# The embedding's product of an attention layer, computed as two products of 64 rows on the two halves of the array

## The chip, the core and the metric

The kernel runs on one core of a Trainium2 chip. The metric is the device time of one execution in microseconds, as the median of several runs; the shorter the better.

## What is computed

One layer: multi-head latent attention with a gated output, and then a per-layer embedding that is gated by the residual stream. All is float32; 1024 tokens, width 1024, an embedding of width 256. The end of it, with which this document deals, is

```
y = mla_mixer(h, cos, sin, ...)              # ends with (o * silu(z)) @ w_out
x = x + y
gate = jax.nn.sigmoid(rmsnorm(x) @ ple_gate[i])
x = x + gate * (p[i] @ ple_proj[i])          # p: 1024 x 256, ple_proj: 256 x 1024
return rmsnorm(x, final_norm)
```

## The kernel before

Tokens are cut into 8 row tiles of 128, features into chunks of 128 partitions. A product in float32 is the sum of three products of exact parts: with a = hi + lo, hi rounded to float32r, it is hi * hi + hi * lo + lo * hi (`pairs` lists the three). So every chunk of 128 contracted features costs three matmuls for each stretch of up to 512 output columns, and each matmul has its own weight load.

The phases are: projections of x, the gate silu(z), attention by pairs of heads, and the last phase from line 695: the out projection (lines 763 to 784) and then, for one row tile after the other, gate, embedding and norm (lines 786 to 819). Only this last loop is touched. For row tile t it does the following.

- `gate_lhs(t + 1)` makes the next tile's stationary operands: the residual `xs` transposed, as `aTh` and `aTl`, and the embedding `p_t`, as `ph` and `pl` (line 759 by way of line 91). From tile 2 on the transposition is made by VectorE and ScalarE, 32 x 32 blocks at a time (`xb`) which are then copied to their places (`xt`, line 132), then cast (line 746) and subtracted (line 91). The buffers of `aTh`/`aTl` alternate between even and odd tiles, so a cast waits until TensorE has done with the tile two before.
- Two halves i of 512 columns: 24 gate matmuls (8 chunks x 3) into a half of `ps_big`. After the first half come the embedding's matmuls for both halves, 2 chunks x 3 x 2 = 12, into two PSUM banks `ps_pj`. The stationary operand is `ph` or `pl`, the moving one a row of `w_p`.
- For each half: ScalarE's sigmoid from `ps_big` into `sg` (line 801), VectorE's `sg = ps_pj * sg` (line 802) and `xs += sg` (line 803), ScalarE's mean square (line 116).
- The norm: `rsqrt` in three Newton steps on VectorE (lines 96 to 107), the scaling of two halves on VectorE (line 817), the output by SyncE's queue.

The last row tile is cut into columns of 512, 256 and 256, and ScalarE scales one of its halves (line 815).

What stands first on an engine is decided by the scheduler of the framework when the program is built: it reorders each engine's instructions, and at run time each engine keeps that order and waits on semaphores. The transposition for a later tile thus stands between the gating steps of an earlier one. All PSUM tiles of one bank (`ps_tr`, `ps_o`, `ps_pj`) share four buffers.

Of the kernel before, what the change touches and what calls it, by code (L numbers as in the profile page):

```python
# [9 lines left out]
F32 = mybir.dt.float32  # L10
# [7 lines left out]
P = 128  # L18
# [10 lines left out]
PLE = 256  # L29
# [16 lines left out]
def _cut(v, bits):  # L46
    """v rounded to a multiple of 2**-bits."""
    return math.floor(v * 2.0 ** bits + 0.5) / 2.0 ** bits
# [3 lines left out]
def mla_ple_kernel(ctx, tc, x, x_t, p_t, pos, norm_g, w_c, w_z, q_norm, w_q, w_r, kv_norm, w_k, w_v,  # L52
                   w_out, ple_proj, ple_gate, final_norm, out):
    """One multi-head latent attention layer with a per-layer embedding gate.

    Products in float32 are carried as sums of exact float32r parts: a = hi + lo with hi = a
    rounded to float32r and lo = a - hi, so that hi*hi + hi*lo + lo*hi has float32's accuracy.
    """
    nc = tc.nc
# [33 lines left out]
    def rsqrt(v, n, name="rs_y", bufs=None):  # L93
        """1 / sqrt(v) of n columns, by Newton's method."""
        half = small.tile([P, n], I32, tag=f"rs_i{n}", name="rs_i", bufs=2)
        V.tensor_scalar(out=half, in0=v.bitcast(I32), scalar1=1, scalar2=None,
                        op0=ALU.logical_shift_right)
        y = small.tile([P, n], F32, tag=f"{name}{n}", name=name, bufs=bufs)
        V.tensor_scalar(out=y.bitcast(I32), in0=half, scalar1=-1, scalar2=0x5F3759DF,
                        op0=ALU.mult, op1=ALU.add)  # L100
        t = small.tile([P, n], F32, tag=f"rs_t{n}", name="rs_t", bufs=2)
        if n == 1:
            h = small.tile([P, 1], F32, tag="rs_h", name="rs_h", bufs=2)
            V.tensor_scalar(out=h, in0=v, scalar1=-0.5, scalar2=None, op0=ALU.mult)
            for _ in range(3):
                V.tensor_scalar(out=t, in0=y, scalar1=y, scalar2=h, op0=ALU.mult, op1=ALU.mult)
                V.scalar_tensor_tensor(out=y, in0=t, scalar=1.5, in1=y, op0=ALU.add, op1=ALU.mult)
            return y
        for _ in range(3):
            V.scalar_tensor_tensor(out=t, in0=y, scalar=-0.5, in1=y, op0=ALU.mult, op1=ALU.mult)  # L110
            V.tensor_tensor(out=t, in0=t, in1=v, op=ALU.mult)
            V.scalar_tensor_tensor(out=y, in0=t, scalar=1.5, in1=y, op0=ALU.add, op1=ALU.mult)
        return y
# [4 lines left out]
    def transposes(dst, src, n):  # L118
        """dst[:, 128 j + r] = src[r, 128 j + :] for n tiles."""
        for j in range(n):  # L120
            nc.tensor.transpose(dst[:, j * P:(j + 1) * P], src[:, j * P:(j + 1) * P], ident)  # L121

    def block_transposes(src, tmp):
        """src's 128 x 128 tiles transposed by 32 x 32 blocks, which are then moved to their rows."""
        n = src.shape[1]
        blk, dst = (z[:, :n] for z in tmp)
        V.transpose(out=blk, in_=src)
        b, d = (z.rearrange("p (k q n) -> p q k n", q=4, n=32) for z in (blk, dst))
        for i in range(4):
            for j in range(4):  # L130
                copy = A.copy if (i + j) % 4 == 1 else V.tensor_copy
                copy(out=d[i * 32:(i + 1) * 32, j], in_=b[j * 32:(j + 1) * 32, i])
        return dst.rearrange("p (k n) -> p k n", n=P)
# [8 lines left out]

    # z^T takes the place of what the first phase reads only once
    zst = ExitStack()
    zT_pool = zst.enter_context(pool("zT"))
    zT = zT_pool.tile([P, KT, S], F32, name="zT")

    # keeps the tensor engine awake while the first loads are under way
    idle = zT[:, 4, :256].bitcast(BF16)
# [16 lines left out]

    # ---------------------------------------------------------------- h, c_q, c_kv, k_rope
    uph = ExitStack()
# [23 lines left out]

    # x^T goes in unscaled: c_q and c_kv are normed anyway, k_rope and z are scaled afterwards
    def load_xT(t, ks=slice(0, KT)):
# [8 lines left out]
    def u_tile(t):  # L203
# [6 lines left out]
        for k in range(KT):  # L210
            for a, b in pairs:
# [4 lines left out]
                nc.tensor.matmul(pk, st, mv[:, k, QL:], start=first, stop=last)  # L216
        # the squares' means are those of c / r, so EPS is divided by r * r with 1 / r / r = msx + EPS
        un = unb[t % 3]
# [47 lines left out]
    def angles():  # L266
        """cos and sin of the positions' angles."""
        rp = uph.enter_context(pool("rope"))
# [15 lines left out]
        def nearest(o, i, s):  # L284
# [6 lines left out]
                        in1=inv.unsqueeze(1).broadcast_to([P, NT, HF]), op=ALU.mult)  # L291
        # the angle is a0 + 4096 (m0 + 1024 m1): a0 loses its turns in radians, m0 and m1 in turns
        nearest(m, ang, 1.0 / 4096)
# [33 lines left out]
        unwind(ang)  # L327
        # half the angle lies within a quarter turn: sin a = 2 s c, cos a = 1 - 2 s s
        ts1(ang, ang, 0.5, ALU.mult)
# [38 lines left out]

    # ---------------------------------------------------------------- silu(z)^T
    att1 = late.enter_context(pool("att1", side="right"))  # L370
# [36 lines left out]
    def project_r(g, hf):  # L407
        """x cos and x sin of four heads, left in DRAM for the rows that they go to."""
        cols = slice(hf * 512, hf * 512 + 512)
        if hf == 0:  # L410
            rq_of[g] = [tc.dram_tile([2, P, S], F32, name=f"rq{g}{z}") for z in "hl"]
        ps = product_q(wr_of[g], hf)
        t = rt_tile("rt").rearrange("p (c n) -> p c n", c=2)
        for n in range(2):
            V.tensor_tensor(out=t[:, n, :], in0=ps, in1=cs[n][:, cols], op=ALU.mult)
        hi = rh_tile("rh").rearrange("p (c n) -> p c n", c=2)
        lo = t.bitcast(F32R)
        A.copy(out=hi, in_=t)
        sub_hi(G, lo, t, hi)
        for z, d in zip((hi, lo), rq_of[g]):  # L420
            nc.gpsimd.dma_start(out=d.rearrange("c p n -> p c n")[:, :, cols], in_=z.bitcast(F32))

    # With q = [x1, x2] and the rotated key [k1, k2], the rotary score is
    # [x1 cos, x2 cos] . [k1, k2] + [x1 sin, x2 sin] . [k2, -k1].
    # The key's 64 rows go on either half, next to the even and the odd heads' other features.
    def rope_key():
# [22 lines left out]
    def spread(src, dst, n):  # L449
        """dst[n m + r, 128 t + :] = src[:, t, r], for 32 rows r or fewer that come over and over."""  # L450
        t, blk = rt_tile("spread"), rh_tile("blk").bitcast(F32)
# [13 lines left out]
    zph = ExitStack()  # L465
    # 1 / rms of x, along the tokens on every partition
    zr = zph.enter_context(pool("zr", reuse_waits="tile"))
# [36 lines left out]

    # ---------------------------------------------------------------- attention
    atts = ExitStack()
    att = atts.enter_context(pool("att"))
    # P^T of two blocks of queries; the last key tile lacks the first block, and stays empty there.
    # Few key tiles share the end of the buffer of many.
    pt_w = [[att.tile([P, n, 2 * P], F32R, name=f"pt{n}{z}") for z in "hl"] for n in (4, 8)]  # L510
# [22 lines left out]
    def odd_k():  # L533
        """The keys of a pair's second head, once those of the pair before are done with."""
        A.copy(out=k_hi[1][NOPE:], in_=kst[NOPE:])
# [60 lines left out]
    def normalise(c, alloc, eng):  # L596
        """The heads of pair c are divided by their sums, brought along the tokens through DRAM."""
        l = sums.pop(c)
# [95 lines left out]

    # ---------------------------------------------------------------- out projection, gate, norm
    fw1 = ctx.enter_context(pool("fw1", side="right", reuse_waits="tile"))
# [24 lines left out]
    def product(ps, st, w, nk, spans):  # L721
        for k in range(nk):
            for a, b in pairs:
                for o, cols in zip(ps, spans):
                    nc.tensor.matmul(o, st[a][:, k, :], w[k][b][:, cols],  # L725
                                     start=k == 0 and a + b == 0, stop=k == nk - 1 and a == 1)

    def out_lhs(t):
# [57 lines left out]
    for t in range(NT):  # L786
# [4 lines left out]
        spans = [slice(*z) for z in zip(edges, edges[1:])]  # L791
        pp = [ps_pj()[:, :z.stop - z.start] for z in spans]
        ms = small.tile([P, 3], F32, tag="ms2", name="ms2", bufs=2)
        for i, cols in enumerate(spans):
            n = cols.stop - cols.start
            po = ps_tr()[:, :n] if i == 2 else ps[:, cols]
            product([po], gl, w_g, KT, [cols])
            if i != 1:
                product(pp[i:i + 2], pl, w_p, PLE // P, spans[i:i + 2])
            sg = fin.tile([P, 512], F32, tag="sg", name="sg", bufs=2)[:, :n]  # L800
            A.activation(out=sg, in_=po, func=AF.Sigmoid, scale=r2[t])
            V.tensor_tensor(out=sg, in0=pp[i], in1=sg, op=ALU.mult)
            V.tensor_tensor(out=xs[:, t, cols], in0=xs[:, t, cols], in1=sg, op=ALU.add)  # L803
# [66 lines left out]
```

## Time and profile before

| | us |
|---|---|
| median of 3 runs | 727.88 |
| lowest and highest run | 727.80, 728.51 |
| span of the profiled execution | 726.3 |
| TensorE busy in that span | 707.7 |
| VectorE busy | 543.8 |
| ScalarE busy | 400.4 |
| GpSimd busy | 198.4 |

The page gives the profiled execution by its span, from the first instruction to the last; its time as the runs have it isn't on it. The busy share of an engine is a mean over phases with different limits. What a change in the last phase is worth is read there: from the chain of work that ended last, from the order in time on each engine with the idle time ahead of an instruction, and from busy times by stretch. In the names, PE is TensorE, PEld its weight loads, DVE VectorE, ACT ScalarE, POOL GpSimd.

### The profile page before, as it was taken

To read this page: it belongs to the slowest core of one execution; us is meant where nothing else is said; L and a number is where in the kernel's file an instruction comes from. 1 tells how busy PE (TensorE), PEld (TensorE's weight loads), DVE (VectorE), ACT (ScalarE), POOL (GpSimd) and SP (SyncE) were. 2 spreads that over 40 slices of the span, in tenths; PEclk is the share of its full clock that TensorE was granted. 3 is DMA by queue.
4 is the path that set the end of the run, shared out by engine and by line. 5 is a ranking of instruction groups with operands and counts; after the bars stand their busy time and mean duration, and the time that the engine had idled before them with its cause. 6 is when DMAs were issued, how large, how long until landed. Compare 5 with 4: busy or idle time off the path is not lost.

```text
span 726.3 us, 11589 instructions
## 1 busy us (share of the span) xinstructions
PE 707.7 (97%) x4031; PEld 614.0 (85%) x4031; DVE 543.8 (75%) x1364; ACT 400.4 (55%) x919; POOL 198.4 (27%) x208
## 2 busy tenths in 40 slices
PE   8999989999999999999999999998999999999995
PEld 7999768888988999888998899887878888888884
DVE  6996994334888988888888888899654258788854
ACT  6751333334777786777768777776553145333322
POOL 0000200223134533563345542165146142000000
PEclk9999999999999999999999999999999999999998
DMA  8710211324102403034120421033474020111101
GB/s 316 279 69 26 71 38 57 103 88 110 38 15 76 148 30 88 16 106 142 34 74 0 168 84 57 4 115 89 139 282 130 1 81 36 44 36 37 59 29 59
DMA packets 25675, 61.32 MB, mean 84 GB/s; under 512 B 4112, under 2 KB 8080, under 8 KB 25616
## 3 DMA queue, kind: packets, MB, share of 16 engines
q1 hardware_dynamic: 23168, 52.19, 22.7%
q0 software_dynamic: 2304, 8.39, 3.1%
q8 instruction: 32, 0.52, 0.3%
q14 instruction: 27, 0.22, 0.1%
q10 hardware_dynamic: 144, 0.00, 0.0%
HBM read 47.92 MB, written 12.65 MB: 83 GB/s over the span
## 4 chain that ended last, share of the span: by engine, by line
PE 86%; DVE 8%; ACT 2%; DMA 2%; issue 1%; SPq 0%; ACTq 0%; DVEq 0%
PE ps_big L725 22%; PE ps_big L583 13%; PE ps_o L635 10%; PE ps_big L487 9%; PE ps_tr L121 8%; PE ps_pj L403 6%; PE ps_big L215 4%; PE ps_pj L725 3%; PE ps_pj L544 3%; PE ps_pj L527 3%; PE ps_big L216 3%; PE ps_o L215 1%; PE ps_pj L216 1%; DVE kt L443 1%; DMA wst<-in_w_out 1%
## 5 line engine op out<-in xcount | busy, mean ns | idle before, releaser
L725 PE MATMUL ps_big<-w,aTh 128*128 128x512 f32 (+1 forms) x480 | 139.1, 390 | 0.0
L725 PEld LDWEIGHTS ps_big<-w,aTh 128*128 128x128 f32 x480 | 89.5, 188 | 20.1
L593 ACT ACTIVATE prob<-ps_big,mx 128x384 f32<-128x384 f32 (+6 forms) x112 | 89.3, 797 | 16.3 <-DVE mx L588 15.6
L588 DVE TENSOR_REDUCE mx<-ps_big 128x1 f32<-128x384 f32 (+6 forms) x112 | 91.6, 818 | 1.8
L121 PE MATMUL ps_tr<-ident,prob 128*128 128x128 f32 x576 | 84.2, 273 | 1.8 <-ACT prob L593 1.8
L725 PE MATMUL ps_big<-w,aTl 128*128 128x512 f32 (+1 forms) x240 | 84.5, 390 | 0.0
L121 PEld LDWEIGHTS ps_tr<-ident,prob 128*128 128x128 f32 x576 | 68.4, 140 | 11.4 <-ACT prob L593 2.6
L91 DVE TENSOR_TENSOR pt8l<-ps_tr,pt8h 128x512 fp32r<-128x512 f32 (+3 forms) x128 | 71.0, 581 | 4.4 <-ACT pt8h L624 3.8
L583 PE MATMUL ps_big<-k_hi,qh 128*128 128x512 f32 (+2 forms) x176 | 67.7, 385 | 0.9 <-ACT prob L593 0.7
L641 POOL TENSOR_TENSOR zT<-o,zT 64x256 f32<-64x256 f32 x56 | 41.0, 734 | 93.6 <-DVE o L639 79.8
L624 ACT CAST pt8h<-ps_tr 128x512 fp32r<-128x512 f32 (+3 forms) x128 | 60.7, 508 | 4.8 <-PE ps_tr L121 4.3
L583 PE MATMUL ps_big<-k_lo,qh 128*128 128x512 f32 (+2 forms) x176 | 61.9, 352 | 0.0
L583 PE MATMUL ps_big<-k_hi,ql 128*128 128x512 f32 (+2 forms) x176 | 61.4, 349 | 0.0
L635 PE MATMUL ps_o<-pt8h,vals 128*128 128x256 f32 x224 | 57.5, 294 | 0.0
L635 PE MATMUL ps_o<-pt8l,vals 128*128 128x256 f32 x224 | 54.9, 282 | 0.0
L725 PEld LDWEIGHTS ps_big<-w,aTl 128*128 128x128 f32 x240 | 45.0, 188 | 10.2 <-POOL aTl L91 0.5
L479 ACT ACTIVATE zh<-zs,g_col 128x128 fp32r<-128x128 f32 x64 | 20.8, 396 | 50.5 <-DMA zs<-in_w_z 38.0
L487 PE MATMUL ps_big<-hT_hi,zl 128*128 128x512 f32 x128 | 41.3, 404 | 4.1 <-DVE zl L480 4.1
L116 ACT ACTIVATE jk<-xs 128x512 bf16<-128x512 f32 (+2 forms) x25 | 18.8, 750 | 44.2 <-DVE xs L803 36.7
L635 PEld LDWEIGHTS ps_o<-pt8l,vals 128*128 128x128 f32 x224 | 42.8, 191 | 0.0
L635 PEld LDWEIGHTS ps_o<-pt8h,vals 128*128 128x128 f32 x224 | 42.6, 190 | 0.0
L624 ACT CAST pt4h<-ps_tr 128x384 fp32r<-128x384 f32 (+3 forms) x64 | 27.1, 425 | 27.4 <-PE ps_tr L121 27.2
(269 smaller groups left out, 1737.7 us busy)
## 6 DMA issues: line engine op xcount, KB each, us to landing
zT<-in_x SPq DMA_DIRECT2D x8, 512.0 KB, 4.9
zs<-in_w_z SPq DMA_DIRECT2D x16, 256.0 KB, 2.7
rlb<-rl SPq DMA_DIRECT2D x32, 128.0 KB, 3.1
wst<-in_w_out SPq DMA_DIRECT2D x8, 512.0 KB, 4.4
xs<-in_x SPq DMA_DIRECT2D x8, 512.0 KB, 7.2
wst<-in_ple_gate SPq DMA_DIRECT2D x8, 512.0 KB, 3.7
out<-xs SPq DMA_DIRECT2D x16, 256.0 KB, 2.0
zT<-in_x_t SPq DMA_DIRECT2D x6, 512.0 KB, 4.1
```

The costliest lines, as they stand in the source:

```text
L91: eng.tensor_tensor(out=lo, in0=src, in1=hi.bitcast(F32), op=ALU.subtract)
L121: nc.tensor.transpose(dst[:, j * P:(j + 1) * P], src[:, j * P:(j + 1) * P], ident)
L215: nc.tensor.matmul(pq, st, mv[:, k, :QL], start=first, stop=last)
L403: nc.tensor.matmul(ps, w[b][:, k, :], (cq_hi, cq_lo)[a][:, k, hf * 512:hf * 512 + 512], start=k == 0 and a + b == 0, stop=k == n - 1 and a ...
L487: nc.tensor.matmul(ps[:, hf * 512:(hf + 1) * 512], wz[k][b], (hT_hi, hT_lo)[a][:, k, hf * 512:(hf + 1) * 512], start=k == 0 and a + b == 0 ...
L583: nc.tensor.matmul(ps[:, off + s0:off + s1], q[a][:, qs], (k_hi, k_lo)[b][e][:, s0:s1], start=a + b == 0, stop=a == 1)
L588: V.tensor_reduce(out=mx, in_=s, axis=AX.X, op=ALU.max, negate=True)
L593: A.activation(out=pr[:, :n], in_=s, func=AF.Exp, bias=mx, scale=1.0, accum_out=l)
L624: A.copy(out=hi[:, j0:j0 + n, half], in_=src)
L635: nc.tensor.matmul(ps[:, :256], w, z[:, j, :], start=j + n == 0, stop=j == last and n == 1)
L641: (V if h >= H - 2 else G).tensor_tensor(out=z, in0=o[top], in1=z, op=ALU.mult)
L725: nc.tensor.matmul(o, st[a][:, k, :], w[k][b][:, cols], start=k == 0 and a + b == 0, stop=k == nk - 1 and a == 1)
```

## The change

For row tiles 0 to 6, a new function `by_halves` takes the place of `product` for the embedding, and is called once for each half of the columns, so it follows the gate's matmuls of either half. It makes two sums in two PSUM banks: the first from partitions 0 to 63 of each chunk, the second from partitions 64 to 127, a matmul of 64 rows for the one and for the other in turn. The matmuls are built as tiles of 64 x 128 of the array, at row 0 and at row 64. The two sums are joined behind the gate: VectorE multiplies the second by `sg` into `sg2`, GpSimd adds that to `xs`, then VectorE multiplies the first by `sg` and adds it. The last row tile stays as it was. The diff also strips comments, which moves line numbers.

```diff
+    def by_halves(st, w, nk, cols):
+        ps = [ps_pj(), ps_pj()]
+        for k in range(nk):
+            for a, b in pairs:
+                for e in range(2):
+                    r = slice(e * P // 2, (e + 1) * P // 2)
+                    nc.tensor.matmul(ps[e], st[a][r, k, :], w[k][b][r, cols],
+                                     start=k + a + b == 0, stop=k == nk - 1 and a == 1)
+        return ps
...
-        pp = [ps_pj()[:, :z.stop - z.start] for z in spans]
+        pp = [ps_pj()[:, :z.stop - z.start] if last else None for z in spans]
...
             product([po], gl, w_g, KT, [cols])
-            if i != 1:
-                product(pp[i:i + 2], pl, w_p, PLE // P, spans[i:i + 2])
+            if last:
+                if i != 1:
+                    product(pp[i:i + 2], pl, w_p, PLE // P, spans[i:i + 2])
+            else:
+                pp[i] = by_halves(pl, w_p, PLE // P, cols)
             sg = fin.tile([P, 512], F32, tag="sg", name="sg", bufs=2)[:, :n]
             A.activation(out=sg, in_=po, func=AF.Sigmoid, scale=r2[t])
-            V.tensor_tensor(out=sg, in0=pp[i], in1=sg, op=ALU.mult)
+            if not last:
+                sg2 = fin.tile([P, 512], F32, tag="sg2", name="sg2", bufs=1)
+                V.tensor_tensor(out=sg2, in0=pp[i][1], in1=sg, op=ALU.mult)
+                G.tensor_tensor(out=xs[:, t, cols], in0=xs[:, t, cols], in1=sg2, op=ALU.add)
+            V.tensor_tensor(out=sg, in0=pp[i] if last else pp[i][0], in1=sg, op=ALU.mult)
             V.tensor_tensor(out=xs[:, t, cols], in0=xs[:, t, cols], in1=sg, op=ALU.add)
```

On TensorE, in row tile 0, the 12 matmuls behind the first half's gate were pairs of column halves (`x2`, of one `w` row each), and are pairs of row halves; w_7113 and w_7114 are the high and low part of the first chunk of `ple_proj`, w_7119 and w_7120 of the second, w_7019 and w_7018 of the gate's last.

```order
 L725 MATMUL ps_big<-w_7019,aTh 128x512
 L725 MATMUL ps_big<-w_7018,aTl 128x512
-L725 MATMUL ps_pj<-w_7113,ph 128x512 x2
-L725 MATMUL ps_pj<-w_7114,ph 128x512 x2
-L725 MATMUL ps_pj<-w_7113,pl 128x512 x2
-L725 MATMUL ps_pj<-w_7119,ph 128x512 x2
-L725 MATMUL ps_pj<-w_7120,ph 128x512 x2
-L725 MATMUL ps_pj<-w_7119,pl 128x512 x2
+L735 MATMUL ps_pj<-w_7113,ph 128x512 x2
+L735 MATMUL ps_pj<-w_7114,ph 128x512 x2
+L735 MATMUL ps_pj<-w_7113,pl 128x512 x2
+L735 MATMUL ps_pj<-w_7119,ph 128x512 x2
```

The same six pairs come a second time behind the second half's gate, where no embedding matmul stood before.

On VectorE, from the scaling of row tile 0 (line 817, now 835) to the second half of row tile 1, it was (numbers tell buffers apart; `xt` 7365 is for tile 3, 7488 for tile 4):

```order
L817 SCALAR_TENSOR_TENSOR xs_6447<-xs_6447,r3_7224,f_bc_6448 128x512 x2
L802 TENSOR_TENSOR sg_7308<-ps_pj_7269,sg_7308 128x512
L91 TENSOR_TENSOR pl_7386<-pin_7387,ph_7385 128x256
L803 TENSOR_TENSOR xs_6447<-xs_6447,sg_7308 128x512
L746 CAST aTh_7362<-xt_7365 128x1024
L91 TENSOR_TENSOR aTl_7363<-xt_7365,aTh_7362 128x1024
L802 TENSOR_TENSOR sg_7338<-ps_pj_7270,sg_7338 128x512
L132 COPY xt_7488<-xb_7487 32x8x32
L803 TENSOR_TENSOR xs_6447<-xs_6447,sg_7338 128x512
L132 COPY xt_7488<-xb_7487 32x8x32 x5
L807 SCALAR_TENSOR_TENSOR ms2_7271<-ms2_7271 128x1
```

and is, in the changed kernel (`xt` 7405 for tile 3, 7548 for tile 4):

```order
L835 SCALAR_TENSOR_TENSOR xs_6447<-xs_6447,r3_7244,f_bc_6448 128x512 x2
L818 TENSOR_TENSOR sg2_7330<-ps_pj_7315,sg_7328 128x512
L820 TENSOR_TENSOR sg_7328<-ps_pj_7314,sg_7328 128x512
L821 TENSOR_TENSOR xs_6447<-xs_6447,sg_7328 128x512
L757 CAST aTh_7402<-xt_7405 128x1024
L91 TENSOR_TENSOR aTl_7403<-xt_7405,aTh_7402 128x1024
L132 COPY xt_7548<-xb_7547 32x8x32 x6
L818 TENSOR_TENSOR sg2_7377<-ps_pj_7362,sg_7375 128x512
L91 TENSOR_TENSOR pl_7426<-pin_7427,ph_7425 128x256
L820 TENSOR_TENSOR sg_7375<-ps_pj_7361,sg_7375 128x512
L132 COPY xt_7548<-xb_7547 32x8x32
L821 TENSOR_TENSOR xs_6447<-xs_6447,sg_7375 128x512
```

Each half has one multiplication more (L818), and its addition to `xs` (L821) waits for GpSimd's, which stands on GpSimd's queue behind L818; `pl` has moved from the first half to the second, and six copies to ahead of the second half.

## Rows read from the trace of the kernel before

**Rows 1.** The page's part 4, the chain that ended last, by engine

```profile
PE 86%; DVE 8%; ACT 2%; DMA 2%; issue 1%; SPq 0%; ACTq 0%; DVEq 0%
```

**Rows 2.** The same chain in order of time: start us, us, what

```profile
593.89 0.87 PE ps_tr L121 x8
...
642.63 11.14 PE ps_big L725 x48
653.77 2.73 PE ps_pj L725 x12
...
714.17 2.83 PE ps_tr L725 x24
717.00 0.72 PE ps_pj L725 x6
```

**Rows 3.** Busy times of one row tile; columns PE, PEld, DVE, ACT, POOL, clock, DMA

```profile
642.63:656.50 13.87, 13.87 (x61) 11.27 (x61) 12.21 (x33) 4.85 (x11) 0.00 (x0) 1.00 0.14 49
```

**Rows 4.** Groups by line and form, 606.53 to 718: us, mean ns, idle us before

```profile
L725 PE MATMUL ps_pj<-w,ph 128*128 128x512 f32 x60 | 16.6, 392 | 0.0
L725 PEld LDWEIGHTS ps_pj<-w,ph 128*128 128x128 f32 x68 | 12.4, 188 | 2.6
```

**Rows 5.** TensorE's matmuls in order of time around a transpose of `rl`

```profile
227.54 0.27 PE L602 MATMUL ps_tr<-ident,rl 128*16 128x128 f32 x1
227.57 0.48 PE L583 MATMUL ps_big<-k_lo,qh 128*128 128x512 f32 x1
227.89 0.41 PE L583 MATMUL ps_big<-k_hi,ql 128*128 128x512 f32 x1
228.13 0.39 PE L583 MATMUL ps_big<-k_hi,qh 128*128 128x512 f32 x1
```

**Rows 6.** The weight load of the matmul at 228.13, in order of time

```profile
227.89 0.19 PEld L583 LDWEIGHTS ps_big<-k_hi,qh 128*128 128x128 f32 x1
```

**Rows 7.** VectorE in order of time, row tile 2: start us, us, [idle before]

```profile
645.38 0.68 DVE L802 TENSOR_TENSOR sg<-ps_pj,sg 128x512 f32<-128x512 f32 x1
645.99 0.42 DVE L91 TENSOR_TENSOR pl<-pin,ph 128x256 fp32r<-128x256 f32 x1
646.32 0.69 DVE L803 TENSOR_TENSOR xs<-xs,sg 128x512 f32<-128x512 f32 x1
648.00 0.69 DVE L746 CAST aTh<-xt 128x1024 fp32r<-128x1024 f32 x1 [1.00 <-PE ps_big L725]
...
651.45 1.47 DVE L132 COPY xt<-xb 32x256 f32<-32x256 f32 x5
...
661.83 0.69 DVE L746 CAST aTh<-xt 128x1024 fp32r<-128x1024 f32 x1 [0.91 <-PE ps_big L725]
```

**Rows 8.** VectorE in order of time, row tiles 5 to 7

```profile
689.57 0.69 DVE L746 CAST aTh<-xt 128x1024 fp32r<-128x1024 f32 x1 [1.90 <-PE ps_big L725]
...
697.98 0.69 DVE L802 TENSOR_TENSOR sg<-ps_pj,sg 128x512 f32<-128x512 f32 x1 [0.71 <-PE ps_pj L725]
...
704.43 0.69 DVE L802 TENSOR_TENSOR sg<-ps_pj,sg 128x512 f32<-128x512 f32 x1 [5.04 <-ACT sg L801]
...
711.32 0.69 DVE L802 TENSOR_TENSOR sg<-ps_pj,sg 128x512 f32<-128x512 f32 x1 [1.12 <-PE ps_pj L725]
712.05 0.69 DVE L803 TENSOR_TENSOR xs<-xs,sg 128x512 f32<-128x512 f32 x1
```

**Rows 9.** ScalarE in order of time, row tile 7

```profile
712.83 0.63 ACT L116 ACTIVATE jk<-xs 128x512 bf16<-128x512 f32 x1 [2.86 <-DVE xs L803]
...
714.21 0.47 ACT L801 ACTIVATE sg<-ps_big,r 128x256 f32<-128x256 f32 x1 [0.65 <-PE ps_big L725]
...
717.04 0.47 ACT L801 ACTIVATE sg<-ps_tr,r 128x256 f32<-128x256 f32 x1 [0.84 <-PE ps_tr L725]
```

**Rows 10.** GpSimd's additions and products of 128 x 512, groups by line and form

```profile
L613 POOL TENSOR_TENSOR zT<-zT,rlb 128x512 f32<-128x512 f32 x14 | 18.2, 1305 | 30.4 <-DMA rlb<-rl 30.2
L810 POOL TENSOR_TENSOR xs<-xs,f_bc 128x512 f32<-128x512 f32 x1 | 1.3, 1288 | 107.2 <-ACT jk L116 107.2
```

## Prediction, made before the changed kernel ran

> **What bounds the kernel now.** I read the page's part on the chain first: TensorE makes up 86% of it [rows 1]. Then the same chain in order of time, over the last phase, which is the one that changes: it alternates between groups of 48 gate matmuls in 11.1 us and of 12 embedding matmuls in 2.73 us, with nothing between them, until 717.7 us, 8.6 us ahead of the end [rows 2]. So a 512-column matmul is paced at 11.1 / 48 = 0.231 us, its weight load included, and a row tile at 60 x 0.231 = 13.87 us. The busy times over one such tile say the same: TensorE busy 13.87 of 13.87 us, at full granted clock, and VectorE already busy for 12.21 of them [rows 3]. The last phase therefore ends when TensorE ends plus a tail of those 8.6 us (gating, norm, scaling, output). Two things can move the time: what TensorE's stream costs, and whether VectorE, with 1.7 us spare in a tile, stays off the end.
>
> **TensorE's part.** Seven of the eight row tiles change (the last keeps the old code). In each, 12 matmuls of 128 rows become 24 of 64 rows, all still 512 columns wide: 84 go, 168 come. If the two halves of the array stream at the same time, a pair costs what one full matmul did, and 84 pairs cost 84 x 0.231 us as before. There is next to nothing to win, since the columns to be streamed on each half are the same: at most the part of 0.231 us that does not grow with the columns, 2 x 0.118 - 0.231 = 0.005 us, 84 times 0.4 us. If they run one after the other, the price is 84 x 0.231 = 19.4 us. No row shows a matmul of fewer than 128 rows, so these are the ends. What rows do show is the pace of an instruction with its weight load: 24 matmuls of 256 columns take 2.83 us [rows 2], 0.118 us each, which is where that 0.118 is from. Two issues in a pair are thus 0.236 us, 0.005 more than the 0.231 that the columns take: 84 x 0.005 = 0.4 us. A weight load lasts 188 ns and a 512-column matmul 392 ns from start to end [rows 4], but a load starts when the matmul before it does, as at 227.89 [rows 5, 6], so neither is paid by itself. Near zero is my choice for this term, because that pace is a row of this engine; the sum keeps 0.4 and 19.4 as ends.
>
> The Trainium skill, "TensorEngine Tiling (Array Packing)", Key Properties, says that different tiles of the array can load weights and multiply in parallel; no run here shows it yet.
>
> **Switching between whole and halved array.** Two blocks in a tile, two switches each: 28 in all. The nearest row is the transpose of `rl` (`128*16`: 16 weight columns instead of 128): it starts at 227.54, the matmul behind it at 227.57, and the next at 227.89 [rows 5]. So that odd shape and one 512-column matmul together take 0.35 us, against 0.231 + 0.109 = 0.34 for an ordinary transpose of that width (eight in 0.87 us, [rows 2]) and one such matmul: 0.01 us for two switches. My bound from above is that a switch empties the array, which leaves it the 0.392 - 0.231 = 0.16 us that a matmul still runs when the next one could start: 28 x 0.16 = 4.5 us. I take 0.01 us for each, 0.3 us in all, by the row that is nearest; TensorE is then 0.4 + 0.3 = 0.7 us later.
>
> The Trainium skill, same page and section, has a rule against this change: changing the tiling mode drains TensorE. By it the term would be the 4.5 us rather than the 0.3. The transpose of `rl` does not agree with it, though it is halved in columns and not in rows.
>
> **VectorE's part.** Each of 14 half tiles gains one multiplication (`sg2`) on VectorE and one addition on GpSimd, and VectorE's last addition now waits for GpSimd. In steady state VectorE issues L802 at 645.38, the embedding's low part at 645.99 and L803 at 646.32 [rows 7]: one multiplication more is 0.61 us. It reports about 0.68 us after its start. The wait from one engine's end to another's start is 0.09 us from VectorE at 712.74 to ScalarE at 712.83 [rows 8, 9]; none to or from GpSimd is short enough to read here, so I take it for that one too. A GpSimd addition or product of this shape takes 1.29 to 1.31 us [rows 10]. With 0.04 to 0.09 us for the way back, the addition can start 0.68 + 0.09 + 1.29 + 0.04 = 2.10 us after `sg2` did, or a little later. In the first half only the other multiplication (0.61) stands between them: stall 2.10 - 1.22 = 0.88 us. In the second, `pl` (0.33) and a copy (1.47 / 5 = 0.29) stand there too [rows 7]: stall 0.26 us. A tile costs VectorE 2 x 0.61 + 0.88 + 0.26 = 2.36 us more. What stands behind these waits on VectorE is the next operand (`aTh`, `aTl`) and the transposes' copies; TensorE needs that operand a tile, 13.87 us, after the cast could start (at 648.00 it is written for the tile after next, [rows 7]), so a lag of half of that stalls nobody. Nor do the PSUM banks: a block takes the two that VectorE emptied for the same half one tile before. The other order of the copies and small steps of `rsqrt` I count at nothing: the same instructions, back to back before as after.
>
> Of 2.36 us, the idle time ahead of the cast covers 0.91 to 1.00 [rows 7]. VectorE falls 1.41 us further behind in each of the four tiles from the cast for row tile 2 to that for row tile 6, and 2.36 - 1.90 = 0.46 by the last cast, for row tile 7 [rows 8]: 6.1 us. After it come 0.61 + 0.55 = 1.16 (tile 5, second half, without the copy) and 2 x 1.49 = 2.98 (tile 6): 10.2 us. Against that stand VectorE's idle times before tile 7's first product, 0.71, 5.04 and 1.12 [rows 8], and, once tile 7's gating alternates between VectorE and ScalarE, ScalarE's 0.65 and 0.84 [rows 9]: 8.4 us. What is left over, 10.2 - 8.4 = **1.9 us** (rounded up), arrives at the tail. It runs beside TensorE's 0.7 us, not behind it: the later of the two sets the end. GpSimd itself is idle here, its 14 additions take 18 us of some 110. ScalarE's order changes little; its square waits for the late addition, and the next sigmoid waits behind that square, which speaks for somewhat more than 1.9 if anything.
>
> **The sum.** The profiled execution has a span of 726.3 us, 1.6 under the median of 727.88 of the runs; what lies around the span I leave as it is. 726.3 + 1.9 = 728.2, and on the median 727.88 + 1.9 = 729.8 us.
>
> **The rivals.** *The lag is absorbed.* If a tile's two stalls come out 0.3 us smaller in sum (handovers quicker than the one of 0.09 us that I read, GpSimd's result there before its 1.29 us are over, as VectorE issues after 0.61 of 0.68), 6 x 0.3 = 1.8 us go, and VectorE's leftover falls to nothing. Then TensorE's 0.7 decides, or 0.0 if its switches and issues are free: 727.9 to 728.6, not slower. It decides from a lag of 1.1 us per tile downwards. For it: the 1.9 us is a small difference of two large sums. Against: each stall is fixed by 1.29 us on GpSimd, which hardly varies. There is no mechanism for more than a trace of a gain: the columns streamed stay.
>
> *A drain at every switch.* 28 x 0.16 = 4.5 us on TensorE; VectorE then has 0.6 us more per tile, and its lag hides beneath: 732.4. For it: nothing in the rows shows a switch in rows. Against: the transpose of `rl`. That is the rule on switches named above.
>
> *The halves overlap only in part.* A weight load that is exposed once or twice in a pair gives 0.188 or 2 x 0.188 us instead of hiding: pairs of 0.231 + 0.109 = 0.34 us, 84 x 0.109 = 9.2 us, up to two loads end to end, 0.376 us, 84 x 0.145 = 12.2 us: 737 to 740. Against: weight loads hide now on the same rows [rows 5, 6].
>
> The Trainium skill, "TensorE: Matmul & The Clock Gate", Part 3, gives 3.07 times for four tiles of 32 rows. An estimate from that page: 4 / 3.07 = 1.30 matmul times for such a pack, 0.30 us for a pair, 5.8 us in all, 733.7. No run here shows it.
>
> *The halves don't overlap at all*, so the change does not do what it says: 19.4 us on TensorE, and VectorE's lag gone, since a tile then lasts 16.6 us: 747.3. For it: nothing in this trace shows two matmuls side by side. Against: loads and matmuls do overlap.
>
> **How the numbers follow.** A measurement here can tell about 0.2%, 1.46 us, from no change. Forecast (halves overlap, VectorE's 1.9 us reaches the end): 0.44, 729.4 to 731.5. Lag absorbed: 0.24, of which 0.02 by a hair faster. Drain: 0.07. Partly: 0.10. One after the other: 0.15. So faster 0.02, same 0.22, slower 0.76. The range leaves out the last rival and goes from 727.6 (no cost, a small gain in the issues) to 741 (two loads exposed): 727.6 to 741.
>
> **What would show it.** Halves that overlap: the 64-row matmuls of a pair start within some tens of ns, six pairs fill 1.4 us, and gate blocks follow without a gap. Switches: the first gate matmul behind a block starts 0.23 us after the block's last pair, not 0.4. VectorE: stalls of 0.9 and 0.3 us on GpSimd, casts that move 1.4 us later per tile and no longer wait for TensorE, TensorE ending at about 718.4 and the span about 1.9 us longer. Wrong would be: 24 matmuls filling 5.5 us, TensorE waiting for an operand or a PSUM bank, or VectorE's casts still waiting for TensorE.

## Result and profile after

The changed kernel takes 737.71 us (median of 4 runs, 736.55 to 740.35) against 727.84 us before (4 runs, 727.05 to 728.51): 1.4% more, ratio 1.014 with a 95% interval of 1.0117 to 1.0162, so some 9.9 us. The forecast was 729.8 us, slower, within 727.6 to 741.0. Direction and range hold; the size is five times the forecast's 1.9 us.

The page of the changed kernel, part 1, busy time by engine, and part 4, the chain by engine, answer to [rows 1]:

```profile
PE 713.6 (97%) x4115; PEld 611.7 (83%) x4115; DVE 555.8 (75%) x1378; ACT 399.5 (54%) x919; POOL 217.2 (29%) x222
```

```profile
PE 72%; DVE 16%; ACT 4%; DMA 3%; issue 3%; POOL 2%; SPq 0%; ACTq 0%; DVEq 0%
```

TensorE was 86% of the chain and is 72%; VectorE has gone from 8% to 16%. VectorE is now what TensorE waits for in part of the phase. In order of time (start us, us, what), where the chain runs on TensorE, from the second half of row tile 5 on, it reads

```profile
691.63 5.84 PE ps_big L725 x24
697.48 1.58 PE ps_pj L735 x12
699.06 5.76 PE ps_big L725 x24
704.82 1.58 PE ps_pj L735 x12
706.40 5.76 PE ps_big L725 x24
712.15 1.58 PE ps_pj L735 x12
713.74 5.77 PE ps_big L725 x24
...
727.27 0.72 PE ps_pj L725 x6
```

against [rows 2]. L735 is the 64-row matmuls: 12 of them, six pairs, take 1.58 us. Six full matmuls at the old pace would take 6 x 0.231 = 1.39, so **the pairs do run side by side**, and 0.19 us is left. A block of 24 gate matmuls takes 5.76 us against 24 x 0.231 = 5.55: again 0.21 too much. Each passage from whole to halved array or back costs about **0.20 us**. The weight loads show where (start us, us, engine, line, what, count, [idle ahead of it]):

```profile
620.65 0.19 PEld L725 LDWEIGHTS ps_big<-w,aTl 128*128 128x128 f32 x1
621.19 0.30 PEld L735 LDWEIGHTS ps_pj<-w,ph 64*128 64x128 f32 x4 [0.35 <-issue]
621.53 0.19 PEld L735 LDWEIGHTS ps_pj<-w,pl 64*128 64x128 f32 x2
621.77 0.41 PEld L735 LDWEIGHTS ps_pj<-w,ph 64*128 64x128 f32 x4
622.23 0.19 PEld L735 LDWEIGHTS ps_pj<-w,pl 64*128 64x128 f32 x2
622.77 0.30 PEld L725 LDWEIGHTS ps_big<-w,aTh 128*128 128x128 f32 x2 [0.36 <-issue]
```

Within a block a load follows the one before with next to no idle time, and starts when the matmul ahead of its own does. At either end of the halved block, 621.19 and 622.77, the load path is idle for 0.35 to 0.36 us with nothing named that it waits for, and the first load of the other shape starts with its own matmul. On TensorE, at the second of these ends:

```profile
622.46 0.39 PE L735 MATMUL ps_pj<-w,pl 64*128 64x512 f32 x2
622.77 0.50 PE L725 MATMUL ps_big<-w,aTh 128*128 128x512 f32 x1
```

The first matmul of the new shape starts some 0.32 us after the last pair instead of 0.23, and with its load inside it lasts 0.50 us instead of 0.39: 0.09 + 0.11 = 0.20 us. The other end shows the same 0.32 us (620.87 to 621.19).

In row tile 0 and in tiles 2 to 5 something else is on top. One row tile of VectorE's cycle, by windows (us, then busy us and count of PE, PEld, DVE, ACT, POOL; clock, DMA, GB/s), to be set against [rows 3]:

```profile
652.20:667.76 15.56, 14.77 (x74) 10.96 (x72) 14.18 (x36) 4.62 (x11) 2.69 (x2) 1.00 0.12 43
```

A tile lasts 15.56 us instead of 13.87, and TensorE is idle in part of it at full clock. The wait is this one, on TensorE:

```profile
659.36 0.39 PE L735 MATMUL ps_pj<-w,pl 64*128 64x512 f32 x2
660.53 0.74 PE L725 MATMUL ps_big<-w,aTh 128*128 128x512 f32 x2 [0.79 <-ACT sg L815]
```

The gate's second half waits for ScalarE's sigmoid of the *first* half. ScalarE at that time:

```profile
659.18 0.63 ACT L116 ACTIVATE jk<-xs 128x512 bf16<-128x512 f32 x1 [2.84 <-DVE xs L821]
659.72 0.19 ACT L116 ACTIVATION_READ_ACCUMULATOR jk<-xs 128x1 f32 x1
659.81 0.67 ACT L815 ACTIVATE sg<-ps_big,r 128x512 f32<-128x512 f32 x1
```

The sigmoid could run as soon as its gate block is done, but stands in ScalarE's order behind a mean square (L116) that waits 2.84 us for VectorE's L821, the last addition to `xs` of the tile before. And VectorE:

```profile
651.59 0.69 DVE L821 TENSOR_TENSOR xs<-xs,sg 128x512 f32<-128x512 f32 x1 [0.68 <-POOL xs L819]
652.20 0.69 DVE L757 CAST aTh<-xt 128x1024 fp32r<-128x1024 f32 x1
...
656.05 0.69 DVE L818 TENSOR_TENSOR sg<-ps_pj,sg 128x512 f32<-128x512 f32 x1
656.66 0.41 DVE L91 TENSOR_TENSOR pl<-pin,ph 128x256 fp32r<-128x256 f32 x1
656.99 0.68 DVE L820 TENSOR_TENSOR sg<-ps_pj,sg 128x512 f32<-128x512 f32 x1
657.70 0.66 DVE L132 COPY xt<-xb 32x256 f32<-32x256 f32 x1
658.40 0.69 DVE L821 TENSOR_TENSOR xs<-xs,sg 128x512 f32<-128x512 f32 x1
```

VectorE runs back to back but for GpSimd's wait, and its cast (652.20, the next at 667.76) waits for nobody, where before it waited 0.9 to 1.0 us for TensorE [rows 7]. So there is a ring: VectorE's late addition holds ScalarE's square, that the sigmoid behind it, that TensorE's next gate block. Why the sigmoid is needed by that block is in the code: both halves' gate sums are parts of one PSUM tile from `ps_big`, and the program makes the second half wait for the reading of the first. The same wait is in the program of the kernel before, where 12 matmuls of 2.73 us [rows 2] between the two gate blocks hid it; now 1.58 us stand there. Over the phase (waiter, whom it waits for: us, times, longest):

```profile
PE ps_big L725 <- ACT sg L815: 3.0, 4, 0.8
DVE xs L821 <- POOL xs L819: 6.0, 9, 0.7
```

From the first gate matmul of the phase to TensorE's last matmul, the kernel before takes 606.29 to 717.72, 111.4 us, and the changed one 607.42 to 727.99, 120.6 us: 9.1 us more. The tail behind is 8.6 and 8.5 us. 28 switches at 0.20 are 5.6 us and the waits 3.0. A wait is counted from a matmul's end, 0.39 us after its start, where the next would have started after 0.32, so four waits are 0.3 more; a fifth, of 0.16 us (644.50 to 644.98 in tile 2), is too short to show as idle time. That makes 9.1. Below, this stretch is given as **phase** beside each time, since the stretch ahead of it, which no diff here touches, starts the phase anywhere from 604.2 to 609.3 us in the profiled executions. A phase is one profiled execution, a time the median of several runs, so the two needn't differ by the same amount.

### The profile page after: what moved, and what is told of

Its sections match the earlier page's. It is cut to its first block, busy times and chain, and to the rows that moved or that the text cites. A ratio compares the mean times of both kernels' runs of the same rounds, so it can differ in the third digit from the quotient of the medians.

```text
span 736.5 us, 11805 instructions
## 1 busy us (share of the span) xinstructions
PE 713.6 (97%) x4115; PEld 611.7 (83%) x4115; DVE 555.8 (75%) x1378; ACT 399.5 (54%) x919; POOL 217.2 (29%) x222
## 4 chain that ended last, share of the span: by engine, by line
PE 72%; DVE 16%; ACT 4%; DMA 3%; issue 3%; POOL 2%; SPq 0%; ACTq 0%; DVEq 0%
PE ps_big L583 13%; PE ps_big L725 10%; PE ps_o L635 10%; PE ps_big L487 9%; PE ps_tr L121 8%; PE ps_pj L403 6%; PE ps_big L215 3%; PE ps_pj L544 3%; PE ps_pj L527 3%; PE ps_big L216 3%; DVE xt L132 3%; PE ps_o L215 1%; POOL w L91 1%; DVE xs L821 1%; PE ps_pj L216 1%
## 5 line engine op out<-in xcount | busy, mean ns | idle before, releaser
L725 PE MATMUL ps_big<-w,aTh 128*128 128x512 f32 (+1 forms) x480 | 140.6, 393 | 3.1 <-ACT sg L815 3.0
L121 PEld LDWEIGHTS ps_tr<-ident,prob 128*128 128x128 f32 x576 | 68.3, 140 | 11.5 <-ACT prob L593 2.7
L116 ACT ACTIVATE jk<-xs 128x512 bf16<-128x512 f32 (+2 forms) x25 | 18.8, 750 | 78.6 <-DVE xs L821 71.2
L819 POOL TENSOR_TENSOR xs<-xs,sg 128x512 f32<-128x512 f32 x14 | 18.7, 1339 | 89.6 <-DVE sg L818 89.6
```

Of the source, the lines that this page charges most:

```text
L725: nc.tensor.matmul(o, st[a][:, k, :], w[k][b][:, cols], start=k == 0 and a + b == 0, stop=k == nk - 1 and a == 1)
```

## Experiments

Two theories. **Two causes**: 5.6 us from the switches, the rest from VectorE's ring through the shared gate tile. **One cause**: a switch is cheap and all is VectorE's added work, or the reverse, all is TensorE's. All kernels start from the changed one; times are medians of runs beside the kernel before on the same chip (727.4 to 728.2 us).

**Whole matmuls, same join.** The two sums are over the two chunks of 128 rows instead of the two halves, so nothing switches.

```diff
-                for e in range(2):
-                    r = slice(e * P // 2, (e + 1) * P // 2)
-                    nc.tensor.matmul(ps[e], st[a][r, k, :], w[k][b][r, cols],
-                                     start=k + a + b == 0, stop=k == nk - 1 and a == 1)
+                nc.tensor.matmul(ps[k], st[a][:, k, :], w[k][b][:, cols],
+                                 start=a + b == 0, stop=a == 1)
```

> The embedding's product again with all 128 rows, six matmuls for each half of the columns as before, but the two chunks of contracted features go to two PSUM banks, so that the join on VectorE and GpSimd and the order of the blocks stay as in the changed kernel. No halved array, no switches. Theory of two parts (a halved block costs TensorE 0.40 us for its two switches, 14 x 0.40 = 5.6 us; and the join holds VectorE 15.55 us in a tile, whose late squares hold up ScalarE's sigmoid and so TensorE's next gate block): without switches VectorE's 15.55 us still stand against TensorE's 13.87, so the time is 5 to 8 us over the kernel before, and TensorE waits more than the 3.0 us of the changed kernel. If the two parts simply add: 3.7 us over before. If switches are all that matters: no more than 2 us over before.

733.88 us, ratio 1.0081 (1.0061 to 1.0102); phase 608.19 to 723.17, +3.5 us. Its chain, in order of time, late in the phase:

```profile
707.77 1.40 PE ps_pj L733 x6
709.16 5.54 PE ps_big L725 x24
```

and its wait, over the phase:

```profile
PE ps_big L725 <- ACT sg L813: 2.4, 4, 0.8
```

Blocks are back at 6 x 0.231 and 24 x 0.231: the 0.2 us belong to the change of shape. But 3.5 us stay, with TensorE waiting for the sigmoid as in the changed kernel: idle time counts from a matmul's end, 0.39 us after its start, where the next would have started after 0.23, so four waits are 2.4 + 4 x 0.16 = 3.0 of the 3.5. So the join alone costs time, though TensorE's own work is the old one. By the time, 6.5 us over the kernel before, the forecast of 5 to 8 us came true, but its reason didn't: TensorE's waits didn't grow, and the phase's 3.5 us are near the 3.7 of parts that simply add. In the profiled execution 1.9 us more lie ahead of the phase (608.19 against 606.29), where the mean granted clock from 400 to 500 us is 0.98, and 1.00 in that of the kernel before.

Two things this run shows beside that. VectorE's order is another one here: the copies stand behind the second half's products, as they did before the change, while in the changed kernel six stand ahead of them. TensorE waits all the same, so the moved copies aren't needed for the wait; how much they add to it in the changed kernel no run shows. And VectorE's casts are 14.9 us apart here, not 15.56.

**Halves without the join.**

```diff
-            if not last:
-                sg2 = fin.tile([P, 512], F32, tag="sg2", name="sg2", bufs=1)
-                V.tensor_tensor(out=sg2, in0=pp[i][1], in1=sg, op=ALU.mult)
-                G.tensor_tensor(out=xs[:, t, cols], in0=xs[:, t, cols], in1=sg2, op=ALU.add)
```

> The halved blocks as in the changed kernel, but the second half's sum is never read: no second multiplication, no addition on GpSimd (this leaves rows 64 to 127 of each chunk out of the embedding for row tiles 0 to 6). Theory of two parts: VectorE has its old load, so TensorE's 28 switches alone remain, 5.6 us over the kernel before, and no wait of TensorE for ScalarE in the steady tiles. If the join were all of it: as before, within 1.5 us. If the halves' own matmuls cost something beyond the switches: above 6.5 us.

735.23 us, 1.0098 (1.0075 to 1.012); phase 607.14 to 724.90, +6.3 us. The blocks are 5.76 and 1.58 us throughout, and VectorE's casts wait for TensorE again:

```profile
664.80 0.69 DVE L757 CAST aTh<-xt 128x1024 fp32r<-128x1024 f32 x1 [1.46 <-PE ps_big L725]
```

Only one wait for the sigmoid (0.5 us) is left, in row tile 0. 5.6 + 0.5 = 6.1: the switches stay when VectorE has no more to do than before. By the time it is 7.8 us over, more than the 5.6 forecast. The wait in row tile 0 thus doesn't need the join, only the shorter cover, and the changed kernel has it too (615.43, 0.61 us).

**A gate bank for each half.** The join stays, the shared tile goes.

```diff
-        ps = ps_big()
...
-            po = ps_tr()[:, :n] if i == 2 else ps[:, cols]
+            po = ps_tr()[:, :n] if i == 2 else ps_big()[:, :n]
```

> The changed kernel, but each half's gate sum gets a PSUM buffer of its own (one of the two of two banks, of which one is used), so the second half's gate matmuls no longer wait for the first half's sigmoid but for the one before that. If TensorE's waits of 0.6 to 0.8 us for a late sigmoid come from this shared buffer, they go, TensorE's tile falls from 15.55 to 14.67 us, and the time is 5.6 to 8 us over the kernel before (VectorE's lag then reaches the tail in part), 2 to 4 us under the changed kernel. If TensorE is held up by VectorE in another way (operand, bank of the embedding): no change against the changed kernel, about 10 us over before.

732.67 us, 1.0079 (1.0054 to 1.0103); phase 604.24 to 721.39, +5.7 us, tail 8.5. TensorE waits for no sigmoid. The chain lies on TensorE nearly throughout and repeats

```profile
698.22 1.58 PE ps_pj L735 x12
699.80 5.76 PE ps_big L725 x24
```

VectorE's casts are still 15.55 us apart, as slow as in the changed kernel: its lag is there and costs nothing once TensorE doesn't depend on the sigmoid. This shows the ring: the lag alone isn't the price, the shared tile is what hands it to TensorE. The time, 5.3 us over the kernel before, is just under the 5.6 to 8 forecast: the lag didn't reach the tail.

**Both taken away**: whole matmuls and own gate banks.

> Whole-array matmuls with the join (as in the first experiment) and each half's gate sum in a PSUM buffer of its own: neither switches nor the shared buffer. TensorE's tile should be 13.87 us throughout, without waits, while VectorE's casts stay 14.9 us apart. If the shared gate buffer was the only way in which the join reached TensorE: the last phase is as long as before, 0 to 1.5 us over the kernel before, its lag absorbed before the end. If VectorE's lag reaches the tail as the prediction had it: 1.9 us or more over before.

728.48 us, 1.0007 (0.9995 to 1.002), as before; phase 605.47 to 716.84, -0.1 us. The four cases of the phase add up:

| | own gate banks | shared gate tile |
|---|---|---|
| no switches | -0.1 | +3.5 |
| 28 switches | +5.7 | +9.1 |

3.5 + 5.7 = 9.2 against 9.1. This is one profiled execution each; by the medians the same four are +0.5, +6.5, +5.3 and +9.9 us and don't add up so well (6.5 + 5.3 = 11.8). Nor is VectorE's work the same in both rows of the table, 14.9 us a tile without switches and 15.6 with them. So the two causes rest on the blocks and waits in each trace, and the close sum is in part luck. The tail is 8.9 us here, 0.3 over that of before: VectorE, 14.88 us a tile, just reaches it.

**One block a tile**: both halves' 24 matmuls together behind the first gate half, 14 switches instead of 28, gate tile shared.

```diff
-            else:
-                pp[i] = by_halves(pl, w_p, PLE // P, cols)
+            elif i == 0:
+                pp = [by_halves(pl, w_p, PLE // P, z) for z in spans]
```

> The changed kernel with both column halves' halved products in one block behind the first half's gate, as the kernel before had them: 14 switches instead of 28, the same matmuls and the same join. Theory of two parts: TensorE's tile costs 13.87 + 0.40 = 14.27 us; the sigmoid of the first half has 3.0 us instead of 1.6 to finish before the second half's gate needs the buffer. VectorE's 15.5 us in a tile then bound, and its lag reaches TensorE later: 3 to 7 us over the kernel before. If the cost goes with the 64-row matmuls and not with switches: 5.6 us and more remain of it, about 8 to 10 us over before.

733.8 us, 1.0084 (1.0057 to 1.0111); phase 605.25 to 722.44, +5.8 us. Undisturbed pieces of its chain:

```profile
699.65 2.95 PE ps_pj L735 x24
702.60 11.36 PE ps_big L725 x48
```

2.95 - 12 x 0.231 = 0.18 and 11.36 - 48 x 0.231 = 0.27: still some 0.2 us an end, so 14 x 0.2 = 2.8 us; 2.2 us are waits for the sigmoid, together 5.0 of 5.8.

**One block a tile, own gate banks.**

> The changed kernel with both column halves' halved products in one block a tile (14 switches) and each half's gate sum in a PSUM buffer of its own. With 0.20 us a switch and no wait for a late sigmoid, TensorE's tile is 13.87 + 0.41 = 14.28 us and the last phase 2.9 us longer than before: 2 to 4 us over the kernel before. If the one block had been slow for another reason than the shared buffer: 5 to 6 us over before, as with one block and the shared buffer.

732.45 us, 1.0056 (1.0035 to 1.0078); phase 607.43 to 723.38, +4.5 us, more than I expected. The gate's blocks start 14.28 us apart at first (630.73, 645.01, 659.28), which is 13.87 + 2 x 0.2. Behind that VectorE comes through by another door, on TensorE:

```profile
686.77 0.49 PE L735 MATMUL ps_pj<-w,ph 64*128 64x512 f32 x1 [0.16 <-DVE sg L817]
687.56 0.72 PE L735 MATMUL ps_pj<-w,ph 64*128 64x512 f32 x3 [0.29 <-DVE sg L819]
```

A block needs all four banks of `ps_pj` at once and waits until VectorE has emptied those of the tile before; this tile is 15.49 us. With fewer switches TensorE runs away from VectorE sooner. 2.8 of switches and 1.2 of this wait (15.49 - 14.28) are 4.0 of 4.5.

**Twice the switches**, without the join: a chunk's 6 matmuls behind every 12 gate matmuls, 56 switches.

```diff
-                pp[i] = by_halves(pl, w_p, PLE // P, cols)
+                pp[i] = [ps_pj(), ps_pj()]
+                for k in range(2):
+                    product([po], gl, w_g, KT, [cols], range(4 * k, 4 * k + 4))
+                    by_halves(pl, w_p, PLE // P, cols, pp[i], [k])
...
```

> The halves without the join (the second half's sum is never read, so rows 64 to 127 are left out of the embedding for row tiles 0 to 6), with each block cut in two: three pairs behind the first four chunks of the gate, three behind the last four. The same matmuls as in the run with halves and no join, but 56 switches instead of 28. If a switch costs 0.20 us: TensorE's tile 13.87 + 8 x 0.20 = 15.5 us, the last phase another 5.7 us longer than in that run, 12 us over the kernel before. If the cost goes with 64-row matmuls: as that run, 6 us over before.

740.37 us, 1.0165 (1.0144 to 1.0186); phase 605.84 to 728.79, +11.5 us, and 56 x 0.20 = 11.2. Its chain:

```profile
705.94 0.89 PE ps_pj L733 x6
706.83 2.99 PE ps_big L725 x12
```

Three pairs, 0.69 us, and 0.20. The price is for each switch, whatever the block's length.

**Halves not in turn**, and **all on one half**, both without the join. In the first the six matmuls of one half come before the six of the other; in the second all 12 use rows 0 to 63.

```diff
-        for k in range(nk):
-            for a, b in pairs:
-                for e in range(2):
-                    r = slice(e * P // 2, (e + 1) * P // 2)
+        for e in range(2):
+            r = slice(e * P // 2, (e + 1) * P // 2)
+            for k in range(nk):
+                for a, b in pairs:
...
```

```diff
-                    r = slice(e * P // 2, (e + 1) * P // 2)
+                    r = slice(0, P // 2)
...
```

> The halves without the join (rows 64 to 127 left out of the embedding for row tiles 0 to 6), but first all six matmuls of the one half, then all six of the other. If matmuls overlap only where neighbours in the order lie on different halves: eleven of twelve run one after the other, a block takes 11 x 0.231 + 0.19 = 2.7 us instead of 1.58, 14 x 1.15 = 16 us more, 22 us over the kernel before. If TensorE finds the pairs itself: 1.6 us a block, 6 us over before.

> The halves without the join, both matmuls of a pair on rows 0 to 63 (so rows 64 to 127 are left out of the embedding for row tiles 0 to 6), two PSUM banks in turn as before. If a pair overlaps because it lies on two halves: now 12 x 0.231 + 0.19 = 3.0 us a block, 20 us more than with two halves, 26 us over the kernel before. If two PSUM banks were enough to overlap, or a 64-row matmul is shorter in itself: 1.6 us a block, 6 us over before.

One run each: 744.95 and 754.36 us, 17.0 and 26.4 over the kernel before; phases +13.9 and +24.9 us. All on one half, as forecast for pairs that need two halves, a block in the chain is

```profile
640.07 2.94 PE ps_pj L735 x12
```

12 x 0.231 + 0.17: a 64-row matmul costs as much as a whole one, and the gain of a pair comes from the two halves alone. Not in turn, the same block is

```profile
639.07 2.16 PE ps_pj L735 x12
```

neither 1.58 nor 2.9 but between, so neither forecast came true. The matmuls of that block, on TensorE:

```profile
639.00 0.73 PE L735 MATMUL ps_pj<-w,ph 64*128 64x512 f32 x2
639.57 0.39 PE L735 MATMUL ps_pj<-w,pl 64*128 64x512 f32 x1
639.58 0.84 PE L735 MATMUL ps_pj<-w,ph 64*128 64x512 f32 x4
640.15 0.50 PE L735 MATMUL ps_pj<-w,pl 64*128 64x512 f32 x2
640.38 0.62 PE L735 MATMUL ps_pj<-w,ph 64*128 64x512 f32 x2
640.84 0.39 PE L735 MATMUL ps_pj<-w,pl 64*128 64x512 f32 x1
```

The seventh matmul of the program, the second half's first (`ph`, 639.58), starts with the third (`pl`, 639.57), ahead of the fourth to sixth: three places ahead of its turn. As I read it, two run alone, then four and four side by side, then two alone: 8 x 0.231 = 1.85 us, 0.2 for the switch and 0.11 by which the second half's first is longer, 2.16 in all. So taking the halves in turn is what makes all six pairs overlap, and "each engine keeps that order" (ahead of the prediction) isn't quite so for TensorE.

**The join's addition on VectorE** instead of GpSimd.

```diff
-                G.tensor_tensor(out=xs[:, t, cols], in0=xs[:, t, cols], in1=sg2, op=ALU.add)
+                V.tensor_tensor(out=xs[:, t, cols], in0=xs[:, t, cols], in1=sg2, op=ALU.add)
```

> The changed kernel with the second half's addition on VectorE instead of GpSimd, so VectorE never waits for GpSimd and its copies run beside nothing. VectorE then pays two operations a half tile, 2 x (0.61 + 0.70) = 2.6 us a tile on 12.92: 15.5 us, as much as with GpSimd (15.56 us measured). So no difference of more than 1 us against the changed kernel, 8.5 to 10.5 us over the kernel before, and casts some 15.5 us apart. If waiting for GpSimd was what made the join dear: casts 14.7 us apart, TensorE without waits, 6 us over before.

739.93 us, 1.0162 (1.0135 to 1.0188), 11.7 us over the kernel before and more than the 8.5 to 10.5 forecast; phase 605.77 to 727.34, +10.1 us, 1.0 more than in the changed kernel. No wait for GpSimd is left, but VectorE's casts are 15.75 us apart instead of 15.56, and TensorE's wait for the sigmoid is

```profile
PE ps_big L725 <- ACT sg L815: 4.1, 5, 1.0
```

So it isn't the handover to GpSimd that makes the join dear: two additions of 0.61 us a tile on VectorE cost about as much as the wait (0.68) and the slow copy (0.38 more, last section) that they save.

No kernel here is faster than the one before.

## Why the prediction was right or wrong

- **Halves overlap** (the base of the forecast): right. Six pairs take 1.39 us of a block.
- **Switches**: wrong, and the larger error. The step took 0.01 us from the transpose of `rl` and, from above, 0.16 us for an emptied array. Measured 0.20 us, 28 x 0.20 = 5.6 us instead of 0.3. The row was the nearest but not near: that matmul uses fewer *columns* of the array, and its weights were loaded ahead as usual (at 227.47, for 227.54); the weights of a matmul on half the *rows* aren't. The bound failed as well: it let the next matmul start as soon as the last one ended, with its weights already there. A weight load of 0.188 us behind that would have made the bound 0.16 + 0.19 = 0.35, and 0.20 lies between the two: 0.09 of a later start and 0.11 of a longer first matmul. The kernel before showed the second part: behind the phase's last transposes, at 606.26 and 606.29, the gate's first load also starts with its own matmul, and two matmuls take 0.72 us where two others take 0.62. The Trainium skill, "TensorEngine Tiling (Array Packing)", Key Properties, says that a change of tiling mode drains TensorE; these traces agree in that each change between 128 and 64 rows costs 0.20 us, but no record shows that the array empties. I gave that rule 0.07 on the strength of one row that differed in the dimension that matters.
- **VectorE's cost of a tile**: about right. Casts moved from 12.92 us of VectorE's own work to 15.56, +2.64 where the step said 2.36. Counted as the step counts, from `sg2`'s start to the last addition's, the first half took 2.08 us (649.51 to 651.59) and the step had 2.10; the 0.68 us of idle time in the row is the same stall, counted from the end of the other product. The second half took 2.35 us (656.05 to 658.40) instead of 2.10: the stall on GpSimd was covered, but by a copy that took 0.66 us beside GpSimd's addition instead of 0.29. That is 0.25 of the 0.28 too little.
- **"A lag of half of that stalls nobody"**: wrong. The step followed only VectorE's operand and VectorE's PSUM banks. It missed TensorE's wait for ScalarE's *reading* of the shared gate tile, which stood in the program and was invisible in the trace because 2.73 us of other matmuls hid it. The change itself took 1.15 us of that cover away, and in row tile 0 that was enough for a wait of 0.6 us, with or without the join. The prediction even named the chain on ScalarE (square, then sigmoid), and stopped before asking who waits for the sigmoid. Price: 3.4 us with the switches (9.1 - 5.7), 3.5 without, of which 0.7 and 0.9 lie in row tile 0.
- **The 1.9 us left over at the tail**: it didn't come. The tail is 8.5 us, before 8.6. Where TensorE pays 0.8 us a tile for switches, VectorE's lag is mostly hidden under it; with whole matmuls and own banks, at 1.0 us of lag a tile, 0.3 us reached the tail. At the full 1.4 us a tile beside an unslowed TensorE it wasn't tried, because the scheduler gave that kernel a VectorE order of 14.88 us a tile.
- **The rivals**: the drain rival had the right cost, a price at every switch, and four fifths of its size (4.5 of 5.6), but it also said that VectorE's lag hides beneath, giving 732.4; own gate banks, where that is true, measured 732.67. The missed wait, 3.4 us of the phase, comes on top. The estimate in a sentence beside the partial overlap, 733.7, came nearer than the forecast, and the 737 to 740 of the partial overlap itself hold the measured time, both for a reason that isn't there: pairs lose nothing, as the blocks of 1.58 us show. So the range held by luck: it reached to 741 for a mechanism that didn't occur.
- **What would show it**: "TensorE waiting for an operand or a PSUM bank" was named as a sign of an error, and it is there. For a switch the sign was a gate block 0.4 us behind the last pair instead of 0.23; it is 0.32 where nothing else waits, and the rest of the price is in the first matmul's length.

## What to carry to other kernels

Halving the array's rows gains nothing for a product that already fills them, and costs 0.20 us for each change of shape: count the changes, put the odd shape into as few blocks as the banks allow, and take the two halves in turn. Before work is taken from between two instructions, look in the program for every wait of the second, also those that the trace shows as zero, and note how long the cover was. When an engine falls behind, follow its result through the in-order queue of the next engine until someone doesn't wait: here VectorE, ScalarE's square, ScalarE's sigmoid, TensorE.

## What was not expected of the hardware

- A switch between 128-row and 64-row matmuls costs 0.20 us in either direction, in blocks of 6, 12 and 24, and leaves the weight load path idle for 0.35 us. The one change in columns that a trace here shows, the transpose of `rl` with 16 weight columns, cost 0.01 us [rows 5].
- TensorE starts matmuls for the idle half about three ahead of their place in the program (639.58 above).
- A 32 x 256 copy of VectorE that falls into GpSimd's addition takes 0.66 us instead of 0.28, and the addition 1.40 instead of 1.29 [rows 10]. On GpSimd, the addition that covers the copy at 657.70:

```profile
656.82 1.40 POOL L819 TENSOR_TENSOR xs<-xs,sg 128x512 f32<-128x512 f32 x1 [5.26 <-DVE sg L818]
```

The mean of VectorE's 72 copies of this form fell when the join's addition moved off GpSimd; in the changed kernel and in that experiment (busy us, mean ns | idle ahead):

```profile
L132 DVE COPY xt<-xb 32x256 f32<-32x256 f32 x72 | 22.4, 311 | 2.4 <-POOL w L91 1.1
```

```profile
L132 DVE COPY xt<-xb 32x256 f32<-32x256 f32 x72 | 20.5, 285 | 2.4 <-POOL w L91 1.1
```

The Trainium skill, "GPSIMD Engine Reference", Key points, says that GpSimd shares its SBUF interfaces with VectorE, and that it contends there with VectorE's instructions that run in a 2-port mode or have two SBUF inputs. These rows agree in that both engines are slower side by side, by 0.38 us for one copy. This copy has one input, and its mode no run here shows, so that the shared interface is the cause, and nothing else of the two engines, stays open.
